# The first matmul of an MLP, on both halves of the tokens together, with seven block products instead of eight for ten of its sixteen weight pairs

## Chip, cores and metric

The kernel runs on one core of one Trainium2 chip. The metric is the device time of one execution in microseconds (us), the median of several runs. The profile is of one execution of the kernel before. In it PE is the matmul engine (PEld its weight loads), DVE, ACT and POOL are the vector, scalar and general engines, and SP issues the transfers.

## What is computed

A trunk of two layers on 1024 tokens of width 1024, in float32. Layer 0 is an mLSTM mixer and an MLP, layer 1 a latent attention and an MLP. Shared keys and values are made from the stream between them.

```python
def sqrelu_mlp(h, w1, w2):
    return jnp.square(jax.nn.relu(h @ w1)) @ w2          # w1 1024 x 4096, w2 4096 x 1024

def reference(...):
    cond = jax.nn.silu(c)
    for l in range(DEPTH):                               # 2
        ada = cond @ ada_w[l] + ada_b[l]
        sh1, sc1, g1, sh2, sc2, g2 = jnp.split(ada, 6, axis=-1)
        h = modulate(rmsnorm(x, norm_g[l, 0]), sh1, sc1)
        y = mlstm_mixer(...) if l < N_A else mla_mixer(h, ..., k_nope, k_rope, v, cos, sin)
        x = x + g1[:, None, :] * rmsnorm(y, norm_g[l, 1])
        h = modulate(rmsnorm(x, norm_g[l, 2]), sh2, sc2)
        y = sqrelu_mlp(h, mlp_w1[l], mlp_w2[l])
        x = x + g2[:, None, :] * rmsnorm(y, norm_g[l, 3])
    return x
```

The change is in the MLP of layer 0 (the "first MLP").

## The kernel before

Activations lie transposed: 128 features on the partitions, tokens along the row, in two halves of 512 tokens (`hfs[0]`, `hfs[1]`). A float32 product is made of three matmuls (`mm3`): each operand is split into a rounded high part and the rest as low part, and low x high, high x low and high x high are added in one PSUM buffer. A weight block of 128 x 1024 goes through `wload`: a transfer into one of four `raw` buffers, ACT casts the high part (L189), DVE subtracts it for the low part (L190), both into `ws` slots (8 of them). A block product here means 512 rows of the depth against 128 columns of the weights and 512 tokens: 4 steps of `mm3`, 12 matmuls of 128x512.

PSUM has three kinds of buffers, two of each: `ps` and `pc` of 512 columns, `pm` of 2 x 512.

The MLP is a list of steps (`mlp`). A `hid` step takes one block of 128 of the 4096 hidden features: 8 steps of `mm3` into `ps` (24 matmuls), then ACT applies relu (L957) and square (L958), and the result is split again (L470 on ACT, L471 on DVE). An `up` step multiplies hidden features with the second weight into `pm`, and DVE adds what comes out to the sum in SBUF (L198). Weights are loaded two steps ahead. Each step has a "within" point in its middle, where other work may be put.

Stages, as the order of the program sets them: the mLSTM; the output projection of half 1; the first MLP on half 0 (profile 498 to about 870 us), with the ada sums of the background (`bg_latent`) beside it; then, as two streams, the first MLP on half 1 with the mixer of layer 1 on half 0 (`mixer1`, `attention_first`); then the last MLP on half 0 with the mixer on half 1 (`attention_second`), and the last MLP on half 1.

`two_streams(dense, other, fill)` writes the two streams: when the other stream yields a number n, n steps of dense are written (0.5 is half a step, up to its "within"), and "align" goes on to the next `hid`. On PE the order is as written; `issue_after` holds it so. `attention_first` works on four pairs of heads. For each pair, `prepare_pair` makes queries, keys and values with the rotary part (L1120 and L1121 swap the halves on PE; L1123, L1124 and L1306 to L1311 on DVE and ACT do the rest); then `attend` takes two blocks of 256 queries (j = 0 and 1): the scores of both heads (L1325 to L1331) go to the two `pm` buffers, softmax runs on DVE (row maxima L1335, L1336) and ACT (exponential L1337, which is the last to read `pm`) and DVE (L1338, L1339), PE transposes the result (L1445) and multiplies it with the values.

Ada sums (`ada_chunk`, L358 and L360 on DVE) multiply a column of the conditioning with the rows of a weight.

## Time and profile before

| | |
|---|---|
| median of 3 runs | 2401.15 us (2399.34 to 2404.07) |
| profiled execution: span | 2395.7 us |
| PE, PEld | 2364.8 us (99%), 1945.5 us (81%) |
| DVE, ACT, POOL | 1550.3 us (65%), 1054.9 us (44%), 18.3 us (1%) |
| transfers | 374.48 MB, mean 156 GB/s |
| 512 KB of MLP weights, from issue to landing | 4.1 us (256 times) |

The span of the profiled execution is its own time; no other time was taken for it, so the sum of a prediction is made against the span, and the 5.45 us between it and the median are carried over. A row of a group has: line, engine, operation, output<-inputs by name, shape, count, then busy time and the mean in ns, then how long the engine sat idle before these instructions and what ended that. PE's matmuls overlap, so their durations don't add up to time; a window's length over its number of matmuls does.

### The profile page before, as it was taken

Reading aid. Unit: us, or ns where it says so; the run is one execution under the profiler, and the core shown is the slowest. Engines: PE = TensorE matmul, PEld = TensorE weight load, DVE = VectorE, ACT = ScalarE, POOL = GpSimd, SP = SyncE. Lnnn points to the kernel's source line nnn. Section 1 sums busy time; section 2 is a strip of 40 time slices with the busy share of each in tenths; the row PEclk is TensorE's granted clock in tenths of the full one; section 3 lists DMA queues with packets and bytes.
Section 4 is the critical chain, followed back from the end, with each engine's and each line's share of the span. In section 5 each row is a group of like instructions: output and inputs, shape, how many; then the busy total and the mean of one; then the engine's idle time right before and its main releaser. Section 6 shows DMA issues by size and latency. Waiting matters only on the chain.

```text
span 2395.7 us, 30518 instructions
## 1 busy us (share of the span) xinstructions
PE 2364.8 (99%) x11621; PEld 1945.5 (81%) x11621; DVE 1550.3 (65%) x2431; ACT 1054.9 (44%) x1712; POOL 18.3 (1%) x91
## 2 busy tenths in 40 slices
PE   7999999999999999999999999999999999999998
PEld 5888888788888887888888877888888888888886
DVE  6667866858656677877764867766566386353345
ACT  4355334655333454444444554344444353443333
POOL 1000000000000000000000000000000000000000
PEclk9999999999999999999999999999999999999999
DMA  8442654544654745545543444864424354354431
GB/s 310 148 143 81 192 178 134 165 132 150 189 171 152 243 138 179 159 160 186 168 137 114 153 162 153 260 240 133 139 97 150 105 167 128 101 189 140 144 99 62
DMA packets 377106, 374.48 MB, mean 156 GB/s; under 512 B 24355, under 2 KB 282464, under 8 KB 376960
## 3 DMA queue, kind: packets, MB, share of 16 engines
q1 hardware_dynamic: 376672, 372.44, 48.9%
q8 instruction: 91, 1.49, 0.3%
q14 instruction: 55, 0.45, 0.1%
q0 software_dynamic: 288, 0.10, 0.0%
HBM read 313.24 MB, written 59.24 MB: 155 GB/s over the span
## 4 chain that ended last, share of the span: by engine, by line
PE 91%; DVE 4%; DMA 3%; ACT 1%; issue 1%; SPq 0%; DVEq 0%; ACTq 0%
PE ps L231 17%; PE ps L232 17%; PE ps L233 17%; PE pm L231 10%; PE pm L232 10%; PE pm L233 10%; PE pc L1445 1%; PE pc L231 1%; PE pc L233 1%; PE pc L232 1%; PE pm L815 1%; PE pm L1331 1%; DMA raw<-in_mlp_w_dram 1%; DVE wl L190 1%; PE pm L1325 1%
## 5 line engine op out<-in xcount | busy, mean ns | idle before, releaser
L190 DVE TENSOR_TENSOR wl<-raw,wh 128x1024 fp32r<-128x1024 f32 (+2 forms) x366 | 438.7, 1202 | 449.5 <-ACT wh L189 442.3
L189 ACT CAST wh<-raw 128x1024 fp32r<-128x1024 f32 (+2 forms) x366 | 376.0, 1032 | 717.0 <-PE ps L231 392.2
L231 PE MATMUL ps<-k,wl 128*128 128x512 f32 x1528 | 611.0, 400 | 2.3 <-ACT k L671 1.4
L233 PE MATMUL ps<-k,wh 128*128 128x512 f32 x1528 | 601.0, 393 | 0.0
L232 PE MATMUL ps<-k,wh 128*128 128x512 f32 x1528 | 600.9, 393 | 0.0
L231 PEld LDWEIGHTS ps<-k,wl 128*128 128x128 f32 x1528 | 287.0, 188 | 69.7 <-issue 2.9
L233 PEld LDWEIGHTS ps<-k,wh 128*128 128x128 f32 x1528 | 287.0, 188 | 67.3 <-issue 0.5
L232 PEld LDWEIGHTS ps<-k,wh 128*128 128x128 f32 x1528 | 287.5, 188 | 63.6 <-issue 1.7
L198 DVE TENSOR_TENSOR k<-k,pm 128x512 f32<-128x512 f32 (+1 forms) x254 | 210.9, 859 | 107.0 <-PE pm L233 106.5
L231 PE MATMUL pm<-hd,wl 128*128 128x512 f32 x512 | 202.0, 394 | 0.4 <-ACT hd L470 0.4
L233 PE MATMUL pm<-hd,wh 128*128 128x512 f32 x512 | 199.8, 391 | 0.0
L232 PE MATMUL pm<-hd,wh 128*128 128x512 f32 x512 | 199.5, 390 | 0.2 <-DVE hd L471 0.2
L231 PE MATMUL pm<-wh,hd 128*128 128x512 f32 x488 | 192.9, 395 | 3.2 <-ACT raw L1337 2.9
L232 PE MATMUL pm<-wl,hd 128*128 128x512 f32 x488 | 191.3, 392 | 0.0
L233 PE MATMUL pm<-wh,hd 128*128 128x512 f32 x488 | 190.3, 390 | 0.0
L360 DVE SCALAR_TENSOR_TENSOR tma<-raw,cond,tma 128x512 f32<-128x512 f32 x168 | 125.6, 747 | 20.6 <-DMA raw<-in_kv_ada_w_dram 14.6
L471 DVE TENSOR_TENSOR hd<-tmp,hd 128x512 fp32r<-128x512 f32 x128 | 88.3, 690 | 56.8 <-ACT hd L470 56.5
L1337 ACT ACTIVATE raw<-pm,sm 128x128 f32<-128x128 f32 (+3 forms) x64 | 47.5, 742 | 151.3 <-DVE sm L1336 122.7
L232 PEld LDWEIGHTS pm<-hd,wh 128*128 128x128 f32 x512 | 96.2, 188 | 21.3 <-DVE hd L471 0.5
L231 PEld LDWEIGHTS pm<-hd,wl 128*128 128x128 f32 x512 | 96.1, 188 | 21.2 <-ACT hd L470 0.8
L233 PEld LDWEIGHTS pm<-hd,wh 128*128 128x128 f32 x512 | 96.1, 188 | 21.1
L231 PEld LDWEIGHTS pm<-wh,hd 128*128 128x128 f32 x488 | 91.6, 188 | 24.9 <-ACT raw L1337 5.5
(347 smaller groups left out, 3414.5 us busy)
## 6 DMA issues: line engine op xcount, KB each, us to landing
raw<-in_mlp_w_dram SPq DMA_DIRECT2D x256, 512.0 KB, 4.1
raw<-in_ada_w_dram SPq DMA_DIRECT2D x80, 512.0 KB, 4.3
raw<-in_a_w_in_dram SPq DMA_DIRECT2D x48, 512.0 KB, 4.1
xs<-k SPq DMA_DIRECT2D x40, 256.0 KB, 4.8
raw<-in_kv_ada_w_dram SPq DMA_DIRECT2D x16, 512.0 KB, 3.8
raw<-in_a_w_out_dram SPq DMA_DIRECT2D x16, 512.0 KB, 4.6
kd<-k SPq DMA_DIRECT2D x32, 256.0 KB, 3.7
vd<-k SPq DMA_DIRECT2D x32, 256.0 KB, 5.0
```

The lines of the kernel that those rows point to most:

```text
L189: nc.scalar.copy(hi[:, :n], r[:, :n])
L190: i = nc.vector.tensor_sub(lo[:, :n], r[:, :n], hi[:, :n].bitcast(F32))
L198: return f(*a, **k)
L231: nc.tensor.matmul(o, ll, rh, start=start, stop=False)
L232: nc.tensor.matmul(o, lh, rl, start=False, stop=False)
L233: pe_last[0] = nc.tensor.matmul(o, lh, rh, start=False, stop=stop)
L360: nc.vector.scalar_tensor_tensor(acc, r[:, kk], cond[:, k : k + 1], acc, ALU.mult, ALU.add)
L471: nc.vector.tensor_sub(lo, u, hi.bitcast(F32))
L815: nc.tensor.matmul(nv[:, r, i], hf.PT[p_][:, r, cs], v[:, 2 * p_ + r], start=g == 0, stop=True,)
L1325: nc.tensor.matmul(o[:, :w], ql, kh, start=True, stop=False)
L1331: nc.tensor.matmul(o[:, :w], qh, kh, start=False, stop=True)
L1337: nc.scalar.activation(pr[:, :n], f, AF.Exp, bias=m, scale=SCALE, accum_out=l)
```

## The change

For six of the 16 pairs of weight blocks (`ALONE`), the first matmul of the first MLP is done as before, for each half by itself (`up_front`), but the hidden tiles are stored to DRAM (`hidd`) instead of being split and kept. For the other ten pairs it is done for both halves at once (`seven`): a pair of weight blocks (two blocks of 128 hidden features x 1024) against two halves of tokens is a product of 2 x 2 blocks, done with Winograd's form of Strassen's scheme in seven block products (`product`) instead of eight, each of depth 512. The operand sums of the weights are made by `load` in five pieces, one after every other product; the operand sums of the tokens (`T` in `kept1`) are made once, in place of half 1's normalised tiles. Products accumulate in `ps` (1, 6, 5, 3), `pc` (2) and `pm` (7, 4); ACT copies intermediate sums out, DVE adds the outputs. `order` interleaves the products of a pair with those of the pair before.

The second matmul reads the hidden tiles back (`fetch`), four blocks a step, for both halves (`stored=True`). The first two blocks of half 1's normalised tokens are stored (`b12`) and read again in the stage after. The background's sums are taken in blocks of 128 x 512 (`thin`), and those that aren't done by then go to the next stage. In the attention of half 0 each of the other stream's steps asks for half as much of the dense stream, as there is less of it there.

`normed_kept` writes the normalised tiles in place and splits them as 128 x 1024; before, they were split as 128 x 512 (L470 to L474). Lines move by 3 (`mm3` is L232 to L234) and more: the scores are L1545 to L1551 and the exponential L1557.

```diff
+    thin = [False]
...
+    def split_wide(hi, lo, u):
+        nc.scalar.copy(hi, u)
+        nc.vector.tensor_sub(lo, u, hi.bitcast(F32))
+    def normed_kept(y, rstd, A, sh, parts):
+        for b in range(4):
+            with paced():
+                for k in (2 * b, 2 * b + 1):
+                    nc.vector.scalar_tensor_tensor(
+                        y[k], y[k], A[:, k : k + 1], rstd, ALU.mult, ALU.mult
+                    )
+                    nc.scalar.activation(y[k], y[k], AF.Identity, bias=sh[:, k : k + 1])
+                if parts[b]:
+                    split_wide(*parts[b], y.t[b])
+            if b % 2:
                 yield 1
...
+    hidd = scratch([2, NF // 2, P, 2 * H], "hidd")
...
+    def up_front(l, hf, pairs):
+        w1, h = mlp_w1[l], hf.h2
+        def hidden(f):
+            def hid(w):
+                pt = ps()
+                for k in range(KD):
+                    if k == KD // 2:
+                        yield "within"
+                    mm3(pt, w[0][:, k], w[1][:, k], h.hi[k], h.lo[k], k == 0, k == KD - 1)
+                s = tmp()
+                with tc.high_priority(PRIO):
+                    nc.scalar.activation(s, pt, AF.Relu)
+                    nc.scalar.activation(s, s, AF.Square)
+                    nc.sync.dma_start(hidd[hf.i, f // 2][:, ts(f % 2, 512)], s)
+            return lambda: wload([(0, 0, wcols(w1, f * P))], P), hid
+        yield from ahead_of([hidden(f) for p_ in pairs for f in (2 * p_, 2 * p_ + 1)])
+    def seven(l, pairs, B, out):
...
+        def load(p_, w):
+            r1, r2 = prompt(raw)(), prompt(raw)()
+            for r, f in ((r1, 2 * p_), (r2, 2 * p_ + 1)):
+                prompt(nc.sync.dma_start)(v(r), wcols(w1, f * P))
+            yield
+            A = prompt(wsplit)(r1, 1024)
+            w[1], w[2] = half(A, 0), half(A, 1)
+            yield
+            with tc.high_priority(PRIO):
+                t1, t2 = raw(), raw()
+                nc.vector.tensor_add(t2[:, lo_], r2[:, lo_], r2[:, hi_])
+                nc.vector.tensor_sub(t1[:, lo_], r1[:, lo_], r2[:, lo_])
+                nc.vector.tensor_sub(t1[:, hi_], t2[:, lo_], r1[:, lo_])
+                nc.vector.tensor_sub(t2[:, hi_], r1[:, hi_], t1[:, hi_])
+            yield
+            A = prompt(wsplit)(t1, 1024)
+            w[7], w[6] = half(A, 0), half(A, 1)
+            yield
+            A = prompt(wsplit)(t2, 1024)
+            w[5], w[3] = half(A, 0), half(A, 1)
+            with tc.high_priority(PRIO):
+                a22 = sb.tile([P, 1024], F32R, tag="ws", bufs=WS, name=f"wa_{next(uid)}")
+                nc.scalar.copy(a22[:, lo_], r2[:, hi_])
+                nc.vector.tensor_sub(a22[:, hi_], r2[:, hi_], a22[:, lo_].bitcast(F32))
+            w[4] = [v(a22)[:, 0:4], v(a22)[:, 4:8]]
+            yield
+        def product(u, i):
+            o = {1: u.b, 6: u.b, 5: u.b, 3: u.b, 2: u.x, 7: u.z, 4: u.z}[i]
+            (wh, wl), (bh, bl) = u.w[i], B[i]
+            for k in range(4):
+                mm3(o, wh[:, k], wl[:, k], bh[k], bl[k], i in (1, 2, 7) and k == 0, k == 3, more=i not in (1, 2, 7))
+            with tc.high_priority(PRIO):
+                if i == 1:
+                    u.s1 = cut(tmc())
+                    nc.scalar.copy(u.s1, u.b)
+                elif i == 2:
+                    u.to = out(u.p_)
+                    nc.vector.tensor_add(u.to.c[0][0], u.s1, u.x)
+                elif i == 6:
+                    u.s16 = cut(tmc())
+                    nc.scalar.copy(u.s16, u.b)
+                elif i == 7:
+                    u.s7 = cut(tmc())
+                    nc.scalar.copy(u.s7, u.z)
+                elif i == 5:
+                    nc.vector.tensor_add(u.to.c[1][1], u.s7, u.b)
+                elif i == 4:
+                    nc.vector.tensor_add(u.to.c[1][0], u.s16, u.z)
+                else:
+                    nc.scalar.activation(u.to.c[0][1], u.b, AF.Relu)
+                    u.to.done()
+        N = B[1][0][0].shape[1]
+        cut = lambda t: t[:, :N]
+        w, prev, then = {}, None, {}
+        for _ in load(pairs[0], w):
+            pass
+        late = iter(())
+        for n in range(len(pairs) + 1):
+            cur, soon = None, iter(())
+            if n < len(pairs):
+                cur = Half()
+                cur.p_, cur.w = pairs[n], w
+                cur.b, cur.x, cur.z = cut(ps()), cut(pc()), cut(pm()[:, 0])
+                if n + 1 < len(pairs):
+                    w = {}
+                    soon = load(pairs[n + 1], w)
+            order = ((cur, 1), (prev, 5), (cur, 2), (prev, 4), (cur, 6), (prev, 3), (cur, 7))
+            for m, (u, i) in enumerate(order):
+                if u:
+                    product(u, i)
+                if m in (0, 2, 4, 6):
+                    next(soon, None)
+                if m == 1:
+                    next(late, None)
+                if u:
+                    yield "hid"
+            prev, late = cur, soon
+    def both_halves(p_):
+        o, s = Half(), [k4v(), hdv()]
+        o.c = [[s[0][:, 0], s[1][:, 0]], [s[0][:, 1], s[1][:, 1]]]
+        def done():
+            nc.vector.tensor_scalar(s[0], s[0], 0.0, None, ALU.max)
+            nc.vector.tensor_scalar(s[1][:, 1], s[1][:, 1], 0.0, None, ALU.max)
+            for i in range(2):
+                nc.scalar.activation(s[i], s[i], AF.Square)
+                nc.sync.dma_start(hidd[i, p_], s[i].rearrange("p a b -> p (a b)"))
+        o.done = done
+        return o
+    home = [k4v]
...
+        def fetch(f):
+            with tc.high_priority(PRIO):
+                r, hi, lo = raw(), home[0](F32R), home[0](F32R)
+                nc.sync.dma_start(r, hidd[hf.i, f // 2])
+                split_wide(hi, lo, r.rearrange("p (a b) -> p a b", b=512))
+            for e in range(2):
+                hids[f + e] = (hi[:, e], lo[:, e])
...
+        if stored:
+            fetch(0)
+            fetch(2)
+            steps = []
+            for g in range(NF // 4):
+                for i in range(4):
+                    load, run = up(list(range(4 * g, 4 * g + 4)), i, g == NF // 4 - 1)
+                    def both(load=load, f=4 * g + 2 * i):
+                        w = load()
+                        if i >= 2 and f < NF:
+                            fetch(f)
+                        return w
+                    steps.append((both, run))
+            n = 0
+            for v in ahead_of(steps, True):
...
-        yield 1
+        yield (0.5, 1)[hf.i]
...
-            yield 2
+            yield 1
...
-        yield 1
+        yield (0.5, 1)[hf.i]
...
-                    yield 1
+                    yield (0.5, 1)[hf.i]
...
-                hf, groups, cycle((1,)),
+                hf, groups, cycle((0.5,)),
...
+    ALONE = 6
...
+    def kept1(y, rstd):
+        part = lambda *a: [alloc(F32R) for alloc in a]
+        b22 = [part(k4v, k4v) for _ in range(2)]
+        yield from normed_kept(y1, rstd, A1, adac(0, SH2), [None, None, *b22])
+        yt, zt = y0.t, y1.t
+        for b in range(2):
+            nc.sync.dma_start(b12[b], wide(zt[b]))
+            nc.vector.tensor_sub(yt[b], zt[b], yt[b])
+            nc.vector.tensor_sub(zt[b], zt[b + 2], zt[b])
+            nc.vector.tensor_sub(zt[b + 2], zt[b + 2], yt[b])
+            nc.vector.tensor_sub(yt[b + 2], yt[b + 2], zt[b + 2])
+        yield 1
+        T = {}
...
+        parts(5, yt[0], hdv, hdv)
+        parts(5, yt[1], hdv, hdv)
+        parts(7, zt[0], hdv, hdv)
+        yield 1
+        parts(7, zt[1], k4v, k4v)
+        parts(6, zt[2], k4v, k4v)
+        parts(4, yt[2], k4v, k4v)
+        yield 1
+        parts(6, zt[3], k4v, hdv)
+        parts(4, yt[3], k4v, k4v)
+        h = hfs[0].h2
+        h0 = list(zip(h.hi.t, h.lo.t))
+        T.update({1: h0[:2], 2: h0[2:], 3: b22})
+        for i, (p_, q_) in T.items():
+            blocks[i] = [[t[:, e] for t in (a, b) for e in range(2)] for a, b in zip(p_, q_)]
...
+    for v in up_front(0, hfs[0], range(ALONE)):
+        if v != "within":
+            next(p1, None)
             next(p1, None)
     drain(p1)
-    two_streams(f0, behind(bg_latent(), 4))
+    bga = chain(bgs, bg_rest())
+    thin[0] = True
+    traced = nc.cur_bb.bb.instructions
+    z0 = FH()
+    f2 = mlp(0, hfs[0], z0, [], stored=True)
+    home[0] = hdv
+    f0, n = seven(0, range(ALONE, NF // 2), blocks, both_halves), 0
+    while go(f0) is not end:
+        pace[0] = next(i for i in reversed(traced) if i.engine == dve)
+        n += 1
+        v = next(bga, "done")
+        if n == 7 * (NF // 2 - ALONE) - 2:
+            next(f2)
...
+    def with_b12(g):
+        for n, v in enumerate(g):
+            if n == 30:
+                hfs[1].h2 = Half()
+                again = [[k4v(F32R), k4v(F32R)] for _ in range(2)]
+                for b in range(2):
+                    r = raw()
+                    nc.sync.dma_start(r, b12[b])
+                    split_wide(*again[b], r.rearrange("p (a b) -> p a b", b=512))
+                hfs[1].h2.hi, hfs[1].h2.lo = (
+                    FH(tiles=[t[i] for t in again + hfs[1].b22]) for i in range(2)
+                )
+            yield v
+    while v != "done":
+        v = next(bga)
+    thin[0] = False
+    drain(bgs)
+    bgl, n = bg_latent(), 0
+    f2 = with_b12(f2)
+    while go(f2) is not end:
+        pace[0] = next(i for i in reversed(traced) if i.engine == dve)
+        n += 1
+        if n % 2:
+            next(bgl, None)
+    drain(bgl)
...
+    def plain_then(g, f):
+        for n, v in enumerate(g):
+            if n == 4 * ALONE - 6:
+                home[0] = k4v
+                next(f)
+            yield v
+        yield from f
+    two_streams(
+        plain_then(up_front(0, hfs[1], range(ALONE)), mlp(0, hfs[1], z1, [], stored=True)),
+        mixer1(hfs[0], z0, attention_first), bga,
+    )
```

97 lines of the change are left out of this document (76 added, 21 removed).

## The prediction

> **What bounds the kernel now.** I read the page of the profile first (busy shares, slices, chain, groups), then the windows of each stage, then the timeline of one pair of heads.
>
> ```profile
> PE 2364.8 (99%) x11621; PEld 1945.5 (81%) x11621; DVE 1550.3 (65%) x2431; ACT 1054.9 (44%) x1712; POOL 18.3 (1%) x91
> ...
> PEclk9999999999999999999999999999999999999999
> ...
> PE 91%; DVE 4%; DMA 3%; ACT 1%; issue 1%; SPq 0%; DVEq 0%; ACTq 0%
> ...
> L190 DVE TENSOR_TENSOR wl<-raw,wh 128x1024 fp32r<-128x1024 f32 (+2 forms) x366 | 438.7, 1202 | 449.5 <-ACT wh L189 442.3
> L189 ACT CAST wh<-raw 128x1024 fp32r<-128x1024 f32 (+2 forms) x366 | 376.0, 1032 | 717.0 <-PE ps L231 392.2
> ...
> L360 DVE SCALAR_TENSOR_TENSOR tma<-raw,cond,tma 128x512 f32<-128x512 f32 x168 | 125.6, 747 | 20.6 <-DMA raw<-in_kv_ada_w_dram 14.6
> L231 PE MATMUL pm<-wh,hd 128*128 128x512 f32 x488 | 192.9, 395 | 3.2 <-ACT raw L1337 2.9
> ```
>
> PE is on 91% of the chain, at full clock. Busy time doesn't give the price of a matmul, since consecutive ones overlap (395 ns each); the windows do. In the next fence each row has the window, then busy time and count for PE, PEld, DVE, ACT and POOL, the granted clock, the DMA share and GB/s.
>
> ```profile
> 498.00:566.00 68.00, 68.00 (x294) 54.80 (x293) 53.57 (x76) 41.86 (x61) 0.55 (x4) 1.00 0.44 138
> 566.00:870.00 304.00, 304.00 (x1340) 248.37 (x1339) 197.14 (x265) 121.71 (x158) 0.00 (x0) 1.00 0.56 176
> ...
> 977.50:1050.00 72.50, 72.22 (x375) 60.28 (x374) 55.47 (x97) 30.91 (x57) 0.82 (x4) 1.00 0.53 168
> 1050.00:1122.00 72.00, 71.90 (x373) 60.05 (x372) 54.81 (x95) 30.96 (x57) 0.82 (x4) 1.00 0.53 169
> 1122.00:1194.50 72.50, 72.13 (x373) 60.25 (x373) 55.35 (x98) 30.96 (x57) 0.82 (x4) 1.00 0.54 168
> ```
>
> The first two rows are the first MLP on half 0: almost nothing but 128x512 matmuls, without a gap. 68.00/294 = 0.231 us from start to start (304.00/1340 = 0.227, where a few records may be of shorter ones). The other three are one pair of heads each in the attention of half 0: PE full, DVE busy 55 of 72.5 us. So a matmul that goes is worth 0.230 us as long as PE stays fed, and the question is where it doesn't.
>
> **Matmuls removed: -27.6 us.** Ten of 16 weight pairs go from 8 block products per pair to 7. A block product is 4 steps of 3 matmuls, so a pair goes from 96 to 84, and 10 x 12 = 120 go. The order of PE confirms it (11403 to 11283 of 128x512). 120 x 0.230 = 27.6.
>
> The Trainium skill speaks against this price: "TensorE: Matmul & The Clock Gate", section "Back-to-back issue gap", gives about 131 ns per 512-column matmul as sustained in a real stream, and 216 ns for one alone. By that rule the gain would be 120 x 0.131 = 15.7 us. The windows here disagree (0.231 for 294 in a row), so the row is taken.
>
> **DVE and ACT work added: nothing, with its cover.** From the order: 50 more DVE sums of 1024 (1.20 us, as L190), 10 + 10 maxima, about +65 us on DVE in all; +33 us on ACT. Among these are fetches that no matmul uses: in `both`, `i` is not bound when the steps are listed, so `if i >= 2` is true at all four calls and each hidden pair is fetched twice: 32 dead transfers, casts (L189's 1.03) and subtractions (1.20). A round of seven products lasts 84 x 0.230 = 19.3 us and brings 3.5 weight subtractions, four half-size sums, four output sums and maxima and an ada piece, some 12.5 us of DVE: 65%, as in the window 566 to 870 (197.14/304). The second product, with dead fetches, comes by the same count to some 74%. Both stay covered; without cover the dead fetches alone cost 32 x 1.2 = 38 us. SP issues 112 more transfers. One issue costs 0.3 us (row below), 34 us over 850. A store of hidden tiles waits in SP's queue for a Square on ACT; behind it stand weight loads for two steps or one round ahead (11 to 19 us). POOL loses eight memsets, off any path. The background sums come in single blocks: the same bytes.
>
> ```profile
> 1035.16 0.31 SPq L211
> ```
>
> **First round of seven: +5 us (0 to 8).** Here DVE takes on the sums and splits of half 1's normalised tiles. DVE, ahead of PE's need (before, then changed; L518 is the low part of a block sum, L2095 and L2096 the sums, L1058 the split of the last weight block):
>
> ```order
> L190 TENSOR_TENSOR wl_5143<-raw_5140,wh_5142 128x1024 [waits DMAHW5_49,PE_49,Activation_49]
> L474 SCALAR_TENSOR_TENSOR k_845_4971<-k_724_4302,ada,k_844_4970 128x512 [waits Activation_49] x2
> L474 SCALAR_TENSOR_TENSOR k_847_4973<-k_725_4303,ada,k_846_4972 128x512 [waits Activation_49] x2
> L474 SCALAR_TENSOR_TENSOR k_849_4975<-k_726_4304,ada,k_848_4974 128x512 [waits Activation_49] x2
> L1085 TENSOR_SCALAR tmc_6158<-tmc_6158 128x512 [waits DVE_49]
> ```
>
> ```order
> L1058 TENSOR_TENSOR wa_5210<-raw_5189,wa_5210 128x512 [waits Activation_49]
> L518 TENSOR_TENSOR k_843_4971<-k_726_4305,k_842_4970 128x1024 [waits Activation_49]
> L2096 TENSOR_TENSOR hd_3283<-hd_3283,k_727_4306 128x1024 [waits DVE_49]
> L518 TENSOR_TENSOR hd_4928<-k_724_4303,hd_4927 128x1024
> L190 TENSOR_TENSOR wl_5254<-raw_5230,wh_5253 128x1024 [waits DMAHW2_49,PE_49,Activation_49]
> L389 SCALAR_TENSOR_TENSOR tma_4298<-raw_5234,cond,tma_4298 128x512 [waits DMAHW7_49]
> L518 TENSOR_TENSOR k_845_4975<-hd_3282,k_844_4974 128x1024 [waits Activation_49]
> L518 TENSOR_TENSOR k_849_4983<-hd_3283,k_848_4982 128x1024 [waits Activation_49]
> L1073 TENSOR_TENSOR k_896_5250<-tmc_5228,pc_5214 128x512 [waits PE_49]
> L389 SCALAR_TENSOR_TENSOR tma_4298<-raw_5234,cond,tma_4298 128x512 [waits DVE_49]
> L518 TENSOR_TENSOR hd_4979<-k_727_4306,k_846_4978 128x1024 [waits DVE_49]
> ```
>
> What moved: the last row makes the low part that product 6 reads 32 matmuls (7.4 us) after the last single step. L1058 stands behind an ACT cast that wants a `ws` slot which that last step frees. So from that moment ACT casts (0.6) and DVE does these rows: 7 x 1.20 + 4 x 0.72 = 11.3, and about 1 of waiting for ACT. 0.6 + 11.3 + 1 - 7.4 = 5.5; I take 5. If other slots come free earlier it is 0, with all rows late 8.
>
> **Attention of half 0: +17 us (6 to 28).** Its steps now take half as many dense matmuls: 96 a pair instead of 192, so a pair shrinks from 72.5 to 72.5 - 96 x 0.231 = 50.3 us. And all dense steps there come from the second product, which accumulates in `pm`, the two PSUM buffers that the scores of the two heads also take. PE after the scores, before and changed:
>
> ```order
> L1330 MATMUL pm_8399<-maskA,identb 128x128
> L1331 MATMUL pm_8399<-k_1381_8142,k_1401_8269 128x256
> L231 MATMUL ps_8435<-k_844_4970,wl_8298 128x512
> L232 MATMUL ps_8435<-k_845_4971,wh_8297 128x512
> L233 MATMUL ps_8435<-k_844_4970,wh_8297 128x512
> ```
>
> ```order
> L1550 MATMUL pm_9768<-maskA,identb 128x128
> L1551 MATMUL pm_9768<-k_1705_9565,k_1720_9671 128x256
> L232 MATMUL pm_9809<-k_1664_9384,wl_9503 128x512 [waits PE_49,Activation_49]
> L233 MATMUL pm_9809<-k_1665_9385,wh_9502 128x512
> L234 MATMUL pm_9809<-k_1664_9384,wh_9502 128x512
> ```
>
> What moved: before, 24 matmuls into `ps` followed the scores; now the matmul behind them waits until ACT has read the first head's scores out of `pm`. When that is, the timeline of one pair tells (start, duration; PE, then ACT):
>
> ```profile
> 980.24 0.36 PE L1331 MATMUL pm<-k,k 128*128 128x256 f32 x1
> 980.45 0.39 PE L231 MATMUL ps<-k,wl 128*128 128x512 f32 x1
> ...
> 997.05 0.48 PE L1331 MATMUL pm<-k,k 128*128 128x512 f32 x1
> 997.37 0.40 PE L231 MATMUL ps<-k,wl 128*128 128x512 f32 x1
> ```
>
> ```profile
> 981.79 0.48 ACT L1337 ACTIVATE raw<-pm,sm 128x256 f32<-128x256 f32 x1 [0.81 <-DVE sm L1336]
> ...
> 983.63 0.47 ACT L1337 ACTIVATE raw<-pm,sm 128x256 f32<-128x256 f32 x1 [0.92 <-DVE sm L1336]
> ...
> 999.09 0.69 ACT L1337 ACTIVATE raw<-pm,sm 128x512 f32<-128x512 f32 x1 [1.87 <-DVE sm L1336]
> ...
> 1003.63 0.68 ACT L1337 ACTIVATE raw<-pm,sm 128x512 f32<-128x512 f32 x1
> ```
>
> The first head's second exponential ends at 982.27 and 999.78. PE could go on at 980.45 and 997.37: waits of 1.8 and 2.4 us, 4.2 a pair, 17 for four pairs. Low end: the wait the trace has for this (`pm` on L1337, 2.9 us over four, so 0.7 each): 8 x 0.7 = 6. High end: each time 1.4 us more, as DVE, whose row maxima stand ahead of each exponential, is busier: 28. DVE's load: by the order, the instructions of a pair come to 52.5 us instead of 60.3, so 55.47 x 52.5/60.3 = 48.3 in 50.3 + 4.2 = 54.5 us, 89% instead of 77%.
>
> **Rotary chain ahead of the scores: +1.5 us (0 to 12).** Between the matmul L1121 that swaps the halves and the scores stood 48 dense matmuls (11 us), now 24 (5.5).
>
> ```profile
> 1038.11 0.39 PE L1121 MATMUL pc<-tmc,selW 128*128 128x512 f32 x1
> ...
> 1049.82 0.39 PE L1325 MATMUL pm<-k,k 128*128 128x256 f32 x1 [0.28 <-DVE k L198]
> ```
>
> ```profile
> 1041.28 0.69 DVE L1123 TENSOR_TENSOR tmc<-pc,hd 128x512 f32<-128x512 f32 x1
> ...
> 1044.28 0.69 DVE L1124 TENSOR_TENSOR tmc<-tmc,tmc 128x512 f32<-128x512 f32 x1
> 1045.65 0.42 DVE L1308 CAST k<-tmp 64x512 fp32r<-64x512 f32 x1 [0.69 <-ACT tmp L1306]
> ...
> 1047.22 0.69 DVE L1311 TENSOR_TENSOR k<-tmc,tmp 64x512 fp32r<-64x512 f32 x1
> ```
>
> From 1038.50 to 1047.91 are 9.4 us, of which the chain's own seven operations (L1306 on ACT among them, 0.6) are some 4.7 with the hops; the rest is other work between them on DVE. So 0 to 9.4 - 5.5 = 3.9 in each of three pairs. I take 0.5, nearer the own time.
>
> **Sum.** -27.6 + 17 + 5 + 1.5 = -4.1. The profiled execution has a span of 2395.7 us, which would become 2391.6; the median of the runs lies 5.45 above that span, so 2401.15 - 4.1 = 2397.0.
>
> **Rivals.** (a) The waits for `pm` shrink to the trace's 0.7 each and the rest is hidden: -27.6 + 6 = -21.6, 2379.5. For it: the chain to the exponential has loose places (ada sums L360 between the row maxima); against it: it was no quicker in the pair shown, where DVE had 23% free. (b) Slower: the rotary chain, at DVE's 89%, is no quicker than before and lies open for 3.9 us in three pairs: +11.7 instead of 1.5 makes +6.1, 2407. For it: before, the last step ahead of the scores already waited for DVE (0.28 on L198). It decides from 3.6 us a pair on (-4.1 - 1.5 + 10.7 = +5). (c) The first round stalls long enough to cost clock:
>
> ```profile
> 20.00:60.00 40.00, 35.39 (x166) 25.07 (x163) 29.97 (x47) 15.51 (x22) 1.14 (x5) 0.91 0.89 299
> ```
>
> Here PE idles 4.6 us of 40 and the clock falls to 0.91 (3.6 us of 40 lost), while it stays at 1.00 in all windows above. With a stall of 8 and 3.6 for the clock it is -27.6 + 17 + 11.6 + 1.5 = +2.5, 2403.5. The Trainium skill (the page named above, "What's actually happening") has the clock halved after an idle window of about 3.4 us, which this row fits. (d) The change doesn't do what it says: DVE's sums set the pace of the rounds. 12.5 us of 19.3 speak against it; at 20 us a round it would give up 7 us, 2404.
>
> **Chances.** Forecast 0.46, a 0.20, b 0.23, c 0.08, d 0.03. A measurement of this kernel tells 0.2% (4.8 us) from no change. The forecast lies near that bound, its own range 2391 to 2403: 0.21 of it faster, 0.23 within, 0.02 slower. With a faster, c and half of d within, b slower: faster 0.41, within 0.32, slower 0.27. The range goes from below (a) to (b) with the stall at 8 and some more waiting: 2376 to 2412.
>
> **What would show it.** In the profile after: 120 matmuls fewer; `pm` waiting for the exponential (now L1557 or near) with 15 to 20 us over eight or more; a gap of some 5 us in PE at the first product 6; pairs of 53 to 56 us; DVE at 65% in the rounds. I'm wrong if the pairs take 51 us (then a) or 58 and more, with scores waiting for DVE (then b), or if PE has gaps in every round.

## The result, and the profile after

The change makes the kernel slower: 2463.65 us (median of 4 runs, 2460.49 to 2466.11) against 2400.24 for the kernel before on the same chip, a ratio of 1.0262 [1.0247, 1.0276]. That is +63.4 us where -4.1 was forecast, outside the range. The profiled execution has a span of 2459.5 us (before 2395.7). If 120 matmuls less are worth the forecast's -27.6 us, 91 us of new stalls have to be found.

From the page of the profile after: busy time by engine, granted clock by slice, shares of the chain, the matmuls of the second product, and the transfer that reads hidden tiles back.

```profile
PE 2368.1 (96%) x11501; PEld 1940.7 (79%) x11501; DVE 1617.0 (66%) x2501; ACT 1085.6 (44%) x1708; POOL 17.4 (1%) x83
...
PEclk9999999999999989989999999999999999999999
...
PE 79%; DVE 9%; DMA 7%; ACT 3%; issue 2%; SPq 0%; ACTq 0%; DVEq 0%
...
L232 PE MATMUL pm<-k,wl 128*128 128x512 f32 x244 | 102.3, 419 | 20.8 <-ACT raw L1557 16.5
...
raw<-hidd SPq DMA_DIRECT2D x64, 512.0 KB, 4.4
```

PE's share of the chain falls from 91% to 79%; DVE goes from 4% to 9%, DMA from 3% to 7%. DVE's share of the span hardly moves (65% to 66%). Two slices of the clock, the 15th and the 18th (860 to 922 and 1045 to 1106 us), fall below 9 tenths, and the page shows `hidd` read 64 times, twice for each of the 32 tiles. By stage (window, busy time and count of PE, PEld, DVE, ACT and POOL, clock, DMA share, GB/s): the first round of seven, the other rounds, the second product of half 0 in two parts, the start of the second stream, and three stretches of the attention of half 0.

```profile
565.00:575.00 10.00, 4.21 (x15) 3.09 (x14) 9.94 (x12) 2.39 (x3) 0.00 (x0) 0.83 0.31 105
575.00:757.00 182.00, 182.00 (x793) 148.05 (x792) 117.78 (x169) 71.72 (x92) 0.00 (x0) 0.99 0.50 164
757.00:870.00 113.00, 108.36 (x470) 88.50 (x468) 83.29 (x95) 57.66 (x59) 0.00 (x0) 0.98 0.77 246
870.00:960.00 90.00, 76.40 (x291) 58.93 (x292) 70.06 (x101) 29.48 (x30) 0.00 (x0) 0.87 0.69 225
960.00:1060.00 100.00, 100.00 (x429) 80.32 (x428) 66.47 (x90) 46.36 (x72) 0.00 (x0) 1.00 0.61 195
1060.00:1114.00 54.00, 43.71 (x190) 34.47 (x190) 40.85 (x66) 23.56 (x35) 0.41 (x2) 0.87 0.74 232
1114.00:1175.00 61.00, 53.77 (x281) 44.70 (x280) 46.60 (x92) 27.43 (x51) 0.82 (x4) 0.95 0.69 217
1175.00:1235.00 60.00, 52.19 (x276) 43.37 (x274) 46.90 (x83) 23.40 (x45) 0.82 (x4) 0.96 0.62 195
```

The rounds of seven are as foreseen: PE full, DVE at 117.78/182 = 65%. The losses lie before them, behind them in the second product (76.40 of 90 us, clock 0.87), and in the attention, where a pair of heads takes 61 us (the matmul behind the scores comes at 1129.42, 1190.24 and 1251.63 us). PE's waits between 500 and 1420 us (what it did, for whom; us in total, times, longest):

```profile
PE pm L232 <- ACT raw L1557: 16.5, 8, 3.0
PE pm L232 <- DVE wl L190: 7.3, 2, 3.8
PE ps L233 <- DVE hd L518: 5.8, 1, 5.8
...
PE pc L232 <- ACT k L499: 4.5, 1, 4.5
PE pm L233 <- DVE hd L518: 4.2, 4, 2.5
PE pm L232 <- ACT hd L517: 4.1, 2, 3.0
```

The forecast waits are there in nearly the forecast size: 16.5 us in 8 for the exponential, 5.8 for the first product 6. They explain a quarter of the 91.

### The profile page after: what moved, and what is told of

It is laid out like the page before. It is cut to its first block, busy times and chain, and to the rows that moved or that the text cites. A ratio compares the mean times of both kernels' runs of the same rounds, so it can differ in the third digit from the quotient of the medians.

```text
span 2459.5 us, 30665 instructions
## 1 busy us (share of the span) xinstructions
PE 2368.1 (96%) x11501; PEld 1940.7 (79%) x11501; DVE 1617.0 (66%) x2501; ACT 1085.6 (44%) x1708; POOL 17.4 (1%) x83
## 4 chain that ended last, share of the span: by engine, by line
PE 79%; DVE 9%; DMA 7%; ACT 3%; issue 2%; SPq 0%; ACTq 0%; DVEq 0%
PE ps L232 14%; PE ps L233 14%; PE ps L234 14%; PE pm L232 8%; PE pm L233 8%; PE pm L234 8%; DMA raw<-hidd 3%; DMA raw<-in_mlp_w_dram 2%; DVE wl L190 1%; PE pc L233 1%; PE pc L232 1%; PE pc L234 1%; PE pc L1665 1%; DVE tma L389 1%; ACT wh L189 1%
## 5 line engine op out<-in xcount | busy, mean ns | idle before, releaser
L190 DVE TENSOR_TENSOR wl<-raw,wh 128x1024 fp32r<-128x1024 f32 (+2 forms) x356 | 426.6, 1201 | 409.4 <-ACT wh L189 365.8
L232 PE MATMUL ps<-k,wl 128*128 128x512 f32 x1328 | 532.0, 401 | 10.4 <-ACT tmp L1685 4.9
L234 PE MATMUL ps<-k,wh 128*128 128x512 f32 x1328 | 522.8, 394 | 0.0
L233 PE MATMUL ps<-k,wh 128*128 128x512 f32 x1308 | 515.2, 394 | 0.0
L232 PEld LDWEIGHTS ps<-k,wl 128*128 128x128 f32 x1328 | 250.1, 188 | 71.5 <-ACT tmp L1685 6.2
L234 PEld LDWEIGHTS ps<-k,wh 128*128 128x128 f32 x1328 | 250.0, 188 | 58.6 <-issue 0.5
L233 PEld LDWEIGHTS ps<-k,wh 128*128 128x128 f32 x1308 | 246.5, 188 | 54.5 <-issue 2.1
L198 DVE TENSOR_TENSOR k<-k,pm 128x512 f32<-128x512 f32 (+1 forms) x226 | 176.9, 814 | 69.9 <-PE pm L234 69.0
L232 PE MATMUL pm<-wh,hd 128*128 128x512 f32 x488 | 192.5, 394 | 1.5 <-ACT raw L1557 1.4
L234 PE MATMUL pm<-wh,hd 128*128 128x512 f32 x488 | 190.5, 390 | 0.0
L232 PE MATMUL pm<-hd,wl 128*128 128x512 f32 x372 | 151.1, 406 | 14.6 <-DVE wl L190 7.3
L233 PE MATMUL pm<-hd,wh 128*128 128x512 f32 x372 | 150.0, 403 | 4.2 <-DVE hd L518 4.2
L234 PE MATMUL pm<-hd,wh 128*128 128x512 f32 x372 | 149.5, 402 | 0.0
L232 PE MATMUL pm<-k,wl 128*128 128x512 f32 x244 | 102.3, 419 | 20.8 <-ACT raw L1557 16.5
L1557 ACT ACTIVATE raw<-pm,sm 128x128 f32<-128x128 f32 (+3 forms) x64 | 47.5, 742 | 146.0 <-DVE sm L1556 123.5
L232 PEld LDWEIGHTS pm<-wh,hd 128*128 128x128 f32 x488 | 91.6, 188 | 22.3 <-ACT raw L1557 3.2
L234 PEld LDWEIGHTS pm<-wh,hd 128*128 128x128 f32 x488 | 91.6, 188 | 20.1 <-issue 0.5
L233 PEld LDWEIGHTS pm<-wl,hd 128*128 128x128 f32 x488 | 91.7, 188 | 19.4 <-issue 0.7
L232 PEld LDWEIGHTS pm<-hd,wl 128*128 128x128 f32 x372 | 72.5, 195 | 34.6 <-issue 9.3
```

Of the source, the lines that this page charges most:

```text
L190: i = nc.vector.tensor_sub(lo[:, :n], r[:, :n], hi[:, :n].bitcast(F32))
L198: return f(*a, **k)
L232: nc.tensor.matmul(o, ll, rh, start=start, stop=False, **m)
L233: nc.tensor.matmul(o, lh, rl, start=False, stop=False, **m)
L234: pe_last[0] = nc.tensor.matmul(o, lh, rh, start=False, stop=stop, **m)
L1557: nc.scalar.activation(pr[:, :n], f, AF.Exp, bias=m, scale=SCALE, accum_out=l)
```

## The experiments

Letters of theories are those that the expectations themselves introduce. The runs come in five groups (e1 to e5; b1 and e6 to e8; e10 and e12; b2, b3 and e15; e16 and e17). Those of a group share a chip and its runs of the kernel before, so every difference is taken against the group's own kernel before (2398 to 2402.5).

**Each suspect alone.** `e1_bound` binds `i`, which ends the second reading of every hidden tile; `e3_t6first` makes the sums of products 6 first; `e4_ps` gives the second product of half 1 `ps` buffers, so that it shares none with the scores; `e5_all` does all three.

```diff
# e1
-                    def both(load=load, f=4 * g + 2 * i):
+                    def both(load=load, f=4 * g + 2 * i, i=i):
# e3 (kept1; parts 5 and 4 follow behind)
-        parts(5, yt[0], hdv, hdv)
-        parts(5, yt[1], hdv, hdv)
+        parts(6, zt[2], k4v, k4v)
+        parts(6, zt[3], k4v, hdv)
         parts(7, zt[0], hdv, hdv)
...
# e4
-                        b2 = pm()
+                        b2 = None if stored and hf.i else pm()
...
-                    pt = b2[:, m % 2]
+                    pt = ps() if b2 is None else b2[:, m % 2]
...
+                    if b2 is None:
+                        accumulate(m, y[m], pt)
```

> The step index is bound, so each pair of hidden tiles is fetched once: 32 transfers of 512 KB, 32 casts and 32 subtractions fewer, and each fetch is asked for three to four steps ahead of its use instead of one. Theory A (the changed kernel loses time because the four raw buffers turn round too slowly: buffer free, transfer of 4 to 5 us, cast, subtraction, each behind other work): the waits of PE on fetched tiles in 757 to 965 us go, 20 to 35 us less there and some more in the next stage; median 2425 to 2440. Rival B (DVE's and ACT's total work or the latent weights prepared beside it set the pace, the dead fetches are harmless): within 5 us of the changed kernel's 2463.65.

> Only the order of the splits of the token sums is changed: those for products 6 and 7, which the first round needs, come before those for 5 and 4, which only the second round needs. Theory: the one gap of 6 us at 573 us and the half-speed clock behind it go, 6 to 8 us less, median about 2457. Rival: the splits wait for the weight slot that ACT's cast wants, in whatever order; no change.

> In the stage of half 1 the second product accumulates in two single ps buffers instead of one double pm buffer, so the matmuls after the scores need no pm buffer. Theory: the 16.5 us that PE waits for the exponential in eight places go, and with them some of the 82 matmuls at half clock in 1060 to 1350 us: 16 to 25 us less, median 2439 to 2448. Rival: ps is taken by the projections, and the wait goes over to those (ps on a copy or a sum): less than 5 us.

> The three edits together (index bound, splits for products 6 and 7 first, ps in place of pm in the stage of half 1). If the three causes are separate, their gains add: 2463.65 less 25, 7 and 20 gives about 2412; if the waits share one cause (the clock that falls after every idle stretch, or raw buffers late everywhere), more than the sum: down to 2385, the median of before less part of the 27.6 us of removed matmuls.

Measured: e1 2427.22 us (before 2399.0; 1.011 [1.0094, 1.0126]); e3 2466.47 (1.0279 [1.0264, 1.0294]); e4 2469.26 (1.0283 [1.0265, 1.0302]); e5 2433.81 (1.014 [1.0125, 1.0155]). Only the index gains: +63.4 becomes +28.2, so the second reading, with the late use that comes of it (see below), costs 35 us; with all three edits it is +34.8, worse than with the index alone. Why so much shows in the chain of the kernel after, at the second product of half 0 (start, duration, what):

```profile
908.02 1.14 DVE k L198
...
909.44 1.14 DVE wl L190
...
910.60 5.04 DMA raw<-hidd
...
915.66 1.05 ACT hd L517
...
916.74 1.24 DVE hd L518
...
918.02 0.79 PE pm L233
918.81 0.43 PE pm L234
919.24 0.43 PE pm L232
```

A subtraction frees one of the four `raw` buffers, and it stood behind an output sum (L198) on DVE; only then can the transfer into the buffer start, and the cast, the subtraction and the matmul come one after the other: 7.4 us from the free buffer (910.58) to PE, in which DVE works 1.24 on it. SP, which issues the transfers, shows the same: between 757 and 960 us it waited 19.4 us (13 times) for L190 and 15.7 us (9 times) for L518, the subtractions that free these buffers, before reads of hidden tiles. ACT's waits between 757 and 960 us, after and then e1:

```profile
ACT hd L517 <- DMA raw<-hidd: 49.5, 18, 4.5
```

```profile
ACT hd L517 <- DMA raw<-hidd: 14.5, 6, 7.5
```

Windows of e1, for the two of the second product above: 858 matmuls in the 203 us instead of 761, at clock 1.00 and 0.98, with DVE as busy as before (151.3 us for 153.4). The 97 matmuls more are, at 0.230, 22 of the 35 us; the rest shows behind these windows.

```profile
757.00:870.00 113.00, 112.19 (x494) 91.83 (x494) 82.17 (x99) 50.71 (x53) 0.00 (x0) 1.00 0.64 210
870.00:960.00 90.00, 83.99 (x364) 68.54 (x363) 69.15 (x97) 29.41 (x34) 0.00 (x0) 0.98 0.72 229
```

With the index bound, each tile is also read three to four steps ahead of its use instead of one. The run doesn't tell fewer reads from earlier reads, and no run gave the kernel another number of `raw` buffers.

The other two edits moved their wait. PE's waits in e3 (500 to 620 us) and in e4 (1060 to 1450 us):

```profile
PE pc L341 <- DVE tma L389: 6.7, 1, 6.7
```

```profile
PE ps L232 <- DVE k L500: 11.0, 6, 4.6
PE ps L232 <- DVE k L198: 6.2, 2, 4.5
```

In e3 the low part of product 6 is in time, and PE waits 6.7 us at the transposes that end an ada part, for an ada sum on DVE: DVE has 9.94 us of work in these 10 (first window of the kernel after), whatever is first. In e4 the exponential holds up nothing, and the same stretch of the attention waits for DVE's splits and sums.

**Cover, start and side work.** `b1_half` is the kernel before with the halved demand for dense work in the attention of half 0, and one thing that goes with it: its ada sums are taken 8 instead of 4 at a time, so that as much is done. `e6_noada` is e1 with e3's order and no ada sums in the first 11 calls of the rounds of seven; `e8_latent` is e1 with the weights of the latent projections and the rotary tables spread over more of the dense work; `e7_hid` is e1 with eight single hidden steps (in `ps`; `h` in the plan) kept for the places behind the scores, and the second product taking two hidden blocks at a time (`u`).

```diff
# b1, in the kernel before (and the same at the other yields)
-            yield 2
+            yield 1
-    two_streams(mlp(0, hfs[1], z1, [2] * 14 + [4]), mixer1(hfs[0], z0, attention_first), bg_rest())
+    two_streams(mlp(0, hfs[1], z1, [2] * 14 + [4]), mixer1(hfs[0], z0, attention_first), bg_rest(), 8)
# e6
-        v = next(bga, "done")
+        for _ in range(0 if n <= 11 else 2 if n > 14 and n % 5 == 0 else 1):
+            v = next(bga, "done")
# e8
-        if n % 2:
+        if n % 5 == 1:
# e7
+    PLAN = "huuhuuhuuhuuu" + 4 * "hhuu"
```

> The kernel before, with one thing of the change alone: the other stream's steps in the attention of half 0 ask for half as much of the dense stream (and the ada sums run twice as many steps per dense step, so that a pair still gets its two). All matmuls stay; what isn't used beside the attention follows after it. Theory A (half the cover is by itself a loss: PE waits for softmax, for the rotary chain, or for DVE at 90%): 10 to 20 us slower than before, 2410 to 2420, with the clock falling in 977 to 1180 us. Rival B (the cover was twice what was needed; what hurts after the change is that all dense matmuls there want pm): within 5 us of before, since here ps steps still follow the scores.

> Index bound, splits for products 6 and 7 first, and the ada sums left out of the first eleven steps of the seven-product stage (made up for by double steps later). When only the order of the splits was changed, the 5.8 us wait moved to the transpose of an ada sum (6.7 us). Theory: DVE has too much work at this place, so both edits together take the gap away: 6 to 9 us less than the 2427.22 with the index bound alone, about 2419. Rival: the gap stays or moves again, to the next of DVE's results; within 3 us of 2427.

> Index bound, and the rotary tables moved from the second product to the seven-product stage, so that the twelve steps of the latent weights spread over the whole second product (one in five half steps instead of one in two). Theory: the waits of 6 us for weights at 912 and 928 us (raw buffers held by the latent weights, which DVE works on for 4 us each) and the half clock behind them go: 8 us less than 2427.22, about 2419. Rival: DVE in the seven-product stage has no room for the tables, the gain is given back there: within 3 us of 2427.

> Index bound, and the dense stream of the stage of half 1 in another order: eight of the twelve single steps of the first product (24 matmuls each into ps) are kept for the places right behind the scores, and the second product begins with the hidden tiles of the seven-product stage, two blocks at a time. Matmuls are the same in number; DVE adds each output twice as often. Theory: the waits for the exponential (17.3 us in eight places) and most of the 81 matmuls at half clock behind them go, and unlike with ps in place of pm nothing else stands in the way: 20 to 28 us less than 2427.22, 2399 to 2407. Rival: DVE, with more adds, becomes what the scores and projections wait for: 2417 or more.

Measured: b1 2448.39 us (before 2398.12; 1.0207 [1.0191, 1.0222]); e6 2416.26 (1.0078 [1.0063, 1.0093]); e8 2423.75 (1.0101 [1.0084, 1.0118]); e7 2434.3 (1.0147 [1.0129, 1.0165]). So halved cover, with the sums beside it, makes the kernel before 50 us slower, with no seven products in it. e6 gains 10 us on e1 (+18.1 against +28.2). Its first round, the same window as above, has PE full beside a DVE that is just as full, but with what PE needs:

```profile
565.00:575.00 10.00, 10.00 (x45) 8.15 (x44) 10.00 (x12) 5.69 (x9) 0.00 (x0) 1.00 0.18 59
```

e8 gains 2.6 us on e1 (+25.6 against +28.2), less than the 5.4 by which e1's own runs differ. In e7 the wait for the exponential is gone and another stands in its place (1060 to 1450 us): PE waits until DVE has emptied `pm`, as e7's own rival had it (2417 or more).

```profile
PE pm L232 <- DVE k L198: 11.9, 8, 4.0
```

**More cover.** `e12_full` is e6 with the demand for dense work as it was before the change; `e10_alone12` and `e10b` do that with 12 pairs done singly (`ALONE = 12`), hidden steps kept for the attention, the second product taking two blocks at a time, and ada sums beside the last single steps; e10b has e8's spreading too; `e15a` is e10b with ada sums twice as fast in the single steps.

```diff
# e12, and the same at the other yields
-            yield 1
+            yield 2
# e10
-    ALONE = 6
+    ALONE = 12
+    PLAN = "hhuhhuhhuhhuuu" + 4 * "huhuhuhu"
# e15a
+            next(bga)
             next(bga)
```

> As e6_noada (2416.26), but in the attention of half 0 the other stream's steps ask for full dense steps again, as before the change: 192 dense matmuls a pair. The 44 dense steps of this stage are then used up when the attention ends, and what follows it there (output projection, residual, norms) has nothing beside it. Theory A (the cover is what the attention lacks; the waits for pm are one face of it): in the attention the waits for pm stay at about 2 us each in eight places, all others and most of the half clock go; 15 to 20 us less there, and 20 to 45 us more behind it, where PE waits for the norms: median 2420 to 2445. Rival B (pm alone is at fault): the pairs lose as much as with half steps, and the total is 2435 or more.

> Twelve pairs as single steps and four as seven products (48 matmuls removed instead of 120, 11.0 us instead of 27.6), full dense steps in the attention as before the change (24 single steps and 32 of the second product, 56 for a need of 55), single steps right behind the scores, hidden tiles of half 1 fetched once and two blocks at a time, splits for products 6 and 7 first and the ada sums taken in the single steps. Theory A (what the removed matmuls cost is cover in the attention; with the cover whole the gain stays): before less 11.0, plus some 5 us for the start of the rounds and the fetches beside the latent weights: 2390 to 2395, ratio 0.996 to 0.998. Rival: the second product's fetches and twice the adds load DVE and the raw buffers so that the stage of half 1 still loses 10 us or more: 2400 or above.

> As e10_alone12, and the rotary tables go beside the last single steps and the seven-product stage, so that the latent weights spread over the whole second product. Theory: 3 to 6 us less than e10_alone12, as the waits for weights beside the latent weights go (e8_latent: 3.5 us less): 2385 to 2391. Rival: no difference.

> As e10b, with the ada sums taken twice as fast in the single steps, so that none are left over for the start of the second product. Theory: the gap of 8 us at 727 us and the half clock behind it go, 8 to 12 us less than 2439.09: 2427 to 2431. Rival: the gap is the first weights and fetches of the second product, which come late whatever else runs; within 4 us of 2439.

Measured: e12 2452.88 us (before 2398.93; 1.0229 [1.0215, 1.0243]); e10_alone12 2445.08 (1.0194 [1.018, 1.0208]); e10b 2439.09 (1.0173 [1.0159, 1.0187]); e15a 2439.76 (before 2399.75; 1.0173 [1.0157, 1.0188]). None helps; e10_alone12 and e10b, expected at 2385 to 2395, missed by about 50 us. In e12 the dense stream runs out and the mixer's end lies open (PE's waits, 1060 to 1450 us), while the waits behind the scores stay:

```profile
PE pc L490 <- DVE tmc L486: 24.6, 2, 21.9
PE pm L232 <- ACT raw L1557: 14.8, 8, 4.1
```

In e10b PE is full for a pair of heads (a window, first fence below, DVE 44 of 70 us), but no ada sum runs in this window any more; from 1040 to 1110 us, with 25 of them, PE is busy 67.33 of 70 us at clock 0.95. Full cover is thus not shown apart from the sums here. The larger losses sit elsewhere: at the start of the second product of half 0 (PE's waits, second fence, 700 to 760 us), and ahead of and behind the attention. PE's waits between 500 and 1600 us sum to 38.5 us, near the 40.2 by which e10b is slower; their causes were not tested one by one. e15a closes the wait at 727 us and has a new one of 5.3 us at 595 us.

```profile
1180.00:1250.00 70.00, 70.00 (x362) 58.84 (x361) 43.66 (x73) 29.74 (x54) 0.82 (x4) 1.00 0.48 144
```

```profile
PE pm L232 <- DVE wl L190: 9.6, 3, 7.7
```

**Without the ada sums.** `b3_nosum` is the kernel before with the last four ada parts of layer 1 set to a constant, `b2_nosum_half` the same with b1's halved demand, `e16_nosum` is e6 with the same parts left out. `e17_f2` keeps all sums and does some of them in the second product of half 0 instead of the attention; the rotary tables move to the rounds of seven.

```diff
# b2, b3, e16
-            yield from ada_part(1, p_)
+            nc.vector.memset(adac(1, p_), 0.1)
# e17
-        if n % 2:
-            next(bgl, None)
+        if n < 28:
+            n % 2 and next(bgl, None)
+        elif n == 28:
+            drain(bgl)
+        elif n < 60:
+            v = next(bga)
```

> The kernel before without the ada sums of the last gates and norms that run beside the attention of half 0 (the four parts are set to a constant): the control for b2_nosum_half. PE is full there anyway, so theory and rival expect the same: 2394 to 2401.

> The same, with the attention of half 0 asking for half dense steps. Theory A (half the cover is too little by itself: softmax, rotary chain and the transposes wait on each other with 22 us of dense matmuls between): 25 to 50 us above b3_nosum, with pairs of 60 us or more instead of the 50 that the matmuls take. Rival B (in b1_half DVE's bursts of ada sums made the loss): less than 15 us above b3_nosum.

> As e6_noada (2416.26), without the ada sums of layer 1's last four parts (set to a constant), so that none run beside the attention of half 0. Theory A (half the cover is worth some 17 us when DVE is free, and the sums make it 44): 15 to 27 us less, 2390 to 2401; the waits for pm go from 18 us towards 10, as the row maxima aren't behind a sum any more. Rival B (pm's waits come from the order of the buffers alone, DVE's load doesn't matter there): less than 8 us less, 2408 or above.

> As e6_noada, with all sums done, but some three of the eight ada chunks taken in the second part of the second product of half 0 instead of beside the attention, and the rotary tables in the seven-product stage. If A holds, a part of e16_nosum's gain shows: 5 to 10 us less than 2416.26. If the sums only move their cost, within 4 us.

| | against its own kernel before | ratio |
|---|---|---|
| cover full, sums left out (b3) | -6.1 us | 0.9974 [0.9965, 0.9983] |
| cover halved, sums left out (b2) | +10.8 | 1.0054 [1.0038, 1.0071] |
| cover halved, sums done (b1) | +50.3 | 1.0207 [1.0191, 1.0222] |
| e6, sums left out (e16) | -15.3 | 0.9938 [0.9922, 0.9955] |
| e6, some sums moved (e17) | +19.7 | 1.0086 [1.0068, 1.0103] |

Against the kernel with full cover and no sums (b3), halved cover costs 16.9 us and the sums cost 6.1; both together cost 56.4 (b1), 33 more than the two apart. b2's 16.9 lies between the two bounds that its expectations set (25 and 15). Where the 33 go, the windows of the two runs show: between 960 and 1235 us PE idles 33.8 us in b1 and 13.9 in b2, and b1's clock is 0.95, 0.91 and 0.94 in the windows that end at 1060, 1114 and 1175 us (by these shares some 14 us lost), where b2's is 1.00. As b1 takes the sums in eights, it doesn't tell sums from bursts of sums; the changed kernel takes them in fours, and there leaving them out gains 33.4 us (+18.1 to -15.3). e17, with all of the work, shows part of it in the attention and loses more elsewhere: from the first pair's second wait for the exponential to the last pair's there are 162.5 us (1116.06 to 1278.59) instead of e6's 172.1 (1096.40 to 1268.51), and the last two pairs, beside which no sum ran any more, take 52 us each (1174.69, 1226.69, 1278.59). But the attention's first such wait comes 19.5 us later (1099.07 for 1079.57): among other things, a wait of 6.5 us for an ada sum came up at 704 us, in the rounds of seven, and 7.1 us for late weights in the second product (e6: 5.0). What the sums do in the attention, the timeline of the kernel after shows (start, duration; DVE, then PE; in brackets the idle time and who ended it):

```profile
1187.65 0.67 DVE L1555 TENSOR_REDUCE sm<-pm 128x1 f32<-128x512 f32 x1
1188.24 0.74 DVE L389 SCALAR_TENSOR_TENSOR tma<-raw,cond,tma 128x512 f32<-128x512 f32 x1
1188.90 0.41 DVE L1559 TENSOR_SCALAR raw<-raw,sm 128x384 f32<-128x384 f32 x1
1189.23 0.15 DVE L1556 TENSOR_SCALAR sm<-sm 128x1 f32<-128x1 f32 x1
1189.29 0.74 DVE L389 SCALAR_TENSOR_TENSOR tma<-raw,cond,tma 128x512 f32<-128x512 f32 x1
```

```profile
1190.24 0.50 PE L232 MATMUL pm<-k,wl 128*128 128x512 f32 x1 [2.48 <-ACT raw L1557]
```

Between a row maximum (L1555) and its negation (L1556), which the exponential wants, stands an ada sum. Without the sums the eight waits shrink from 18.0 us (e6) to 8.2 (e16), 960 to 1350 us:

```profile
PE pm L232 <- ACT raw L1557: 18.0, 8, 3.4
```

```profile
PE pm L232 <- ACT raw L1557: 8.2, 8, 1.3
```

A stretch of about a pair, e6 and then e16, shows that more than the 10 us of waits went:

```profile
1138.00:1197.00 59.00, 52.57 (x277) 43.73 (x277) 45.61 (x87) 22.04 (x43) 0.82 (x4) 0.97 0.57 182
```

```profile
1138.00:1195.00 57.00, 54.62 (x302) 46.19 (x302) 38.61 (x73) 25.88 (x51) 0.82 (x4) 1.00 0.40 127
```

25 matmuls more in 2 us less, and the clock is back at 1.00; e16's pairs take 52 us (1084.59, 1136.58, 1188.55 and 1240.45). Leaving out the sums leaves out their transfers too (DMA share 0.57 and 0.40), which go through the same `raw` buffers as the weights and the hidden tiles; how much of the gain is theirs was not told apart.

## Why the prediction was wrong

The account, each row against its own kernel before:

| | us |
|---|---|
| 120 matmuls fewer (the forecast's price, not measured alone) | -27.6 |
| second reading of hidden tiles, and later use (after to e1) | +35.2 |
| start of the rounds of seven (e1 to e6) | +10.1 |
| ada sums beside the thinner attention (e6 to e16, less b3's 6.1) | +27.3 |
| what is left, so that it adds up | +18.4 |
| measured | +63.4 |

The last row is a remainder, and the waits of PE that e16 still has between 500 and 1420 us sum to about the same: 8.2 for the exponential, 6.9 for weights, 3.8 in small ones. That these waits are the remainder was not tested.

- **Matmuls, right in the price where PE is fed and in e16's sign.** The rounds of seven ran at 182.00/793 = 0.230 us a matmul, as forecast, and 120 went (11621 to 11501). e16, with no dead reads, a clean start and no sums, is 15.3 us faster than the kernel before, 9.2 if b3's 6.1 are taken off for the sums that it lacks. No kernel with all of the work beat the kernel before.
- **"DVE and ACT work added: nothing, with its cover": the step that failed first.** The dead reads were found, counted (32) and priced by DVE's share, 74%, as covered. DVE's share was right (153.35 of 203 us, 76%), and so was the work added (66.7 us on DVE for 65); the price was not: 35.2 us. By the chain and SP's waits the four `raw` buffers were the limit, each occupied through transfer, cast and subtraction, and the transfer starts only when a buffer is free. A page of averages cannot show this, the chain does. Without cover the prediction had 38 us; that 35.2 is near it is chance, as the 38 were time on DVE, and DVE is as busy in e1.
- **First round of seven, +5: the wait was right (5.8 us in the place named), its cost not.** The start as a whole was worth 10.1: after the 5.8 us the next 11 matmuls started 0.43 us apart (573.57 to 578.26; the clock of that window is 0.83), 2.2 us more, and the rest was not followed. Rival (c) had put the whole stage at 11.6, and at 0.08.
- **Attention of half 0, +17: right in the wait (16.5 in 8, 17 forecast), wrong in what else waits.** The sum of the waits is near in part by luck: 4.2 a pair were forecast, three pairs had 4.4 to 5.4, and the last, beside which no ada sum ran, 1.95, as in e16's last three. Pairs took 61 us instead of 54.5. DVE's work per pair was forecast well (48.3 us, 46.6 in the window from 1114), but it was let be late only at the exponential and, for 0.5 us a pair, in the rotary chain. With the ada sums in among row maxima, splits and output sums other waits came beside it, and a pause near 2 us could cost clock (0.95 and 0.96 in the windows of the pairs). The prediction had seen the sums between the row maxima, but only as slack, in rival (a), and priced them at nothing; b1, b2 and b3 show that thin cover and side work together cost more than the two apart, and e6 to e16 gives 27.3 us for it here.
- **Rotary chain, +1.5:** 2.1 us over three waits of the scores for L198. Rival (b) is out, although pairs of 58 us and more were its sign: the scores wait too little for it. So is (a), since the waits didn't shrink, and (d), since the rounds ran full.

## What the runs showed of the hardware

Pauses far shorter than those of the first round cost clock. PE in the kernel after, behind the scores of a pair, then in e16 at the same kind of place:

```profile
1169.75 0.39 PE L1545 MATMUL pm<-k,k 128*128 128x256 f32 x1 [1.14 <-DVE k L198]
...
1173.36 0.79 PE L232 MATMUL pm<-k,wl 128*128 128x512 f32 x1 [1.89 <-ACT raw L1557]
1173.95 0.63 PE L233 MATMUL pm<-k,wh 128*128 128x512 f32 x1
1174.38 0.63 PE L234 MATMUL pm<-k,wh 128*128 128x512 f32 x1
```

```profile
1136.58 0.50 PE L232 MATMUL pm<-k,wl 128*128 128x512 f32 x1 [1.34 <-ACT raw L1557]
1136.91 0.39 PE L233 MATMUL pm<-k,wh 128*128 128x512 f32 x1
```

After pauses of 1.14 and 1.89 us with 1.7 us of matmuls between them, the next 11 start 0.43 us apart, so the second pause costs 2.2 us more than its length; after 1.34 us they start 0.23 apart. Of ten pauses of 1.7 to 4.6 us between 1060 and 1300 us in the kernel after, six were followed by 7 to 13 such starts and four (1.74 to 2.48 us) by none; all four of 1.3 in e16 by none. So the length of the last pause alone doesn't decide. The Trainium skill, "TensorE: Matmul & The Clock Gate", section "Wait — 56ns, not 53.3ns?", gives 426.7 ns between the starts of 512-column matmuls at half clock, and the runs agree (0.43). The Trainium skill, section "What's actually happening" of the same page, puts the loss after an idle window of about 3.4 us; here it came after a pause of 1.89 behind one of 1.14, and also after single ones of 1.80 (1093.25) and 2.08 us (1273.38), and for this kernel the measurement decides.

## What to carry to other kernels

A busy share does not price a transfer with work behind it: follow the staging buffer round (free, transfer, cast, subtraction, matmul) and ask how many of these turns the pool has room for. Before taking dense matmuls away from beside a dependent chain, list what else stands on the chain's engine: less cover and side work cost 17 and 6 us apart and 56 together here. And a wait that one edit removes has moved, not gone, if the engine behind it is full in that window; look at that engine first.
